# ScalarE in place of SyncE as the issuer of the crossbar transposes in the second FFN

## The chip, the core and the metric

The kernel runs on one core of a Trainium2 chip. The metric is the device time of one execution in microseconds (us). The engines are TensorE (PE, with its weight loads listed apart as PEld), VectorE (DVE), ScalarE (ACT), GpSimd (POOL) and SyncE (SP). Each works through its own instructions in order, and they wait for one another by semaphores. DMAs are issued by an engine's instruction and carried out by 16 DMA engines.

## What is computed

One conformer-like block in float32 on 256 tokens of width 2048: a feed-forward network (FFN), a mixer of differential attention and a causal convolution, and a second FFN. Each is normalised, scaled and shifted with values computed from `c` and `w_ada`.

```
def swiglu(h, w_gu, w_down):
    gu = jnp.einsum('bsd,df->bsf', h, w_gu)
    g, u = jnp.split(gu, 2, axis=-1)
    return jnp.einsum('bsf,fd->bsd', jax.nn.silu(g) * u, w_down)
...
ada = jnp.einsum('bd,de->be', c_act, w_ada[l]) + b_ada[l]
sh1, sc1, g1, shm, scm, gm, sh2, sc2, g2 = jnp.split(ada, N_MOD, axis=-1)
...
h = modulate(rms_norm(x, ffn2_norm[l]), sh2, sc2)
x = x + FFN_RESIDUAL_WEIGHT * g2[:, None, :] * swiglu(h, ffn2_w_gu[l], ffn2_w_down[l])
```

The hidden width of an FFN is 5632. The change is in the second FFN.

## The kernel before

**Weights.** All weights come from memory as float32 tiles of 128 x 2048 (1 MB), which SP loads into the four buffers `raw` (L294, L542). `w_tile` splits each half of a tile into a high and a low part: ACT casts it to `whi` (L305), DVE subtracts to get `wlo` (L307); both have four buffers. `mm3` then makes three matmuls for each product: high times high (L329), high times low (L333), low times high (L334). Half a tile is used by 12 matmuls of 512 columns. So PE needs an ACT cast and a DVE subtraction for every 12 matmuls, and a buffer comes free for the next cast when its 12 matmuls are done.

**The first half of the second FFN.** The 5632 hidden columns are cut into 22 chunks of 256 gate and 256 up columns. The products of a chunk's first of four tiles are made ahead and kept in `parts` (chunks 3, 4 and 5 two of four); the rest are made by a loop over `groups`, first chunks 0, 1 and 2 together, then one chunk at a time, three tiles each (chunks 3, 4 and 5 two). When a chunk's matmuls are done, and the first tile of the next group has been put out, `finish` runs for both token halves: DVE adds the two sums (L830), ACT takes the SiLU (L831), DVE multiplies by the up half (L832).

**The transposes.** The products must be transposed before they can be the stationary operand of the second half. The first FFN does it on PE (`CROSSBAR[0]` is False). The second (`CROSSBAR[96]` is True) uses the DMA engines: ACT splits the product's 32-bit words into two planes of 16 bits (L836, tile `planes`); one tile of instructions later, `rest` has a DMA transpose all eight 128 x 128 blocks of a chunk at once into `turned` (L842); ACT puts the planes together again (L845), casts to the high part (L350), and DVE subtracts to get the low part (L351). In the profile `planes`, `turned` and the result of L845 are all called `tmp`. So each chunk has a line of dependent work L830, L831, L832, L836, L842, L845, L350, L351 over DVE, ACT, the DMA engines, ACT and DVE.

**Fillers.** The remaining `w_ada` rows are loaded into the same `raw` buffers (L192) and reduced on DVE (L193), one for every two weight tiles while any are left (to about 1465 us).

**The order.** The order of each engine's instructions is fixed when the program is built, by a scheduler that simulates the engines with its own costs, in the order and with the priorities in which the code is written. Which engine issues a DMA is part of what it schedules, so moving an issue can move other instructions as well. The second half of the FFN (`down_strassen`) starts after the last chunk.

Of the kernel before, what the change touches and what calls it, by code (L numbers as in the profile page):

```python
# [82 lines left out]
def block_kernel(ctx: ExitStack, tc: tile.TileContext, x_in, pos_in, w_ada, small, w_gu1, w_dn1,  # L83
                 w_in, w_out, w_gu2, w_dn2, out):
    nc = tc.nc
# [18 lines left out]
    def blk(shape, dtype=F32):  # L104
        return blkp.tile(shape, dtype, tag="blk", name=nm("blk"))

    def tmp(shape, dtype=F32):
        return tmpp.tile(shape, dtype, tag="tmp", name=nm("tmp"))
# [7 lines left out]
    def tp_tile(shape=(P, 512)):  # L116
        return tpp.tile(list(shape), F32, tag="tp", name=nm("tp"))
# [53 lines left out]
    def after_tiles(n, fn):  # L171
        later.append([n, fn])
# [176 lines left out]
    def split_from_psum(tp, hi, lo):  # L349
        nc.scalar.copy(out=hi, in_=tp)  # L350
        nc.vector.tensor_sub(out=lo, in0=tp, in1=hi.bitcast(F32))  # L351
# [287 lines left out]
    def ffn(st, w_gu, w_dn, gate_base, ada_a, ada_b, nxt, again, early, early_3):  # L639
# [187 lines left out]
        def finish(c, accs):  # L827
            p = parts[c]
            for t in range(NT):
                nc.vector.tensor_add(out=p[:, t, :], in0=accs[t], in1=p[:, t, :])  # L830
                nc.scalar.activation(out=p[:, t, :256], in_=p[:, t, :256], func=AF.Silu)  # L831
                nc.vector.tensor_mul(out=p[:, t, 256:], in0=p[:, t, :256], in1=p[:, t, 256:])  # L832

            if CROSSBAR[base]:
                planes = tmp([P, 2, NT, 256], U16)
                nc.scalar.copy(out=planes, in_=p[:, :, 256:].bitcast(U16).rearrange("p t (f b) -> p b t f", b=2))  # L836

            def rest():
                a = blk([P, 2, 2, S], F32R)
                if CROSSBAR[base]:  # L840
                    turned = tmp([P, 2, NT, 2, P], U16)
                    nc.sync.dma_start_transpose(out=turned.rearrange("p b t i s -> p (b t i) s"),  # L842
                                                in_=planes.rearrange("p b t f -> p (b t f)"))
                    src = tmp([P, 2, NT, P])
                    nc.scalar.copy(out=src.bitcast(U16).rearrange("p i t (s b) -> p b t i s", b=2), in_=turned)  # L845
                    src = src.rearrange("p i t s -> p i (t s)")
                else:
                    src = tp_tile((P, 2, S))
                    for t in range(NT):
                        for i in range(2):  # L850
                            nc.tensor.transpose(src[:, i, t * P:(t + 1) * P],
                                                p[:, t, 256 + i * P:256 + (i + 1) * P], ident)
                split_from_psum(src, a[:, 0], a[:, 1])
                aT[c] = a

            after_tiles(1, rest)
# [613 lines left out]
```

## Time and profile before

| | |
|---|---|
| runs before: median, lowest, highest | 1826.58, 1826.22, 1826.65 us |
| profiled execution: time, and span from first to last instruction | 1831.11, 1829.3 us |
| granted TensorE clock, mean | 0.999 |
| L842 in the profile | 22 issues by SP, first at 1295.3, last at 1596.8 us |
| ACT, L845 in all | 22, mean 1355 ns, 51.2 us of idle time ahead of them |
| ACT casts of weights (L305) | 581, mean 1044 ns (nearly all 128 x 1024) |
| DVE subtractions (L307) | 581, mean 1210 ns |
| DVE reduction of a `w_ada` row (L193) | 142, mean 2285 ns |

Times in the profile's views are us from the span's start. A row of the order of time gives start, length, engine, line, operation, tile written and tiles read, and in brackets how long the engine stood idle before it and what ended that; rows with x2 or x3 put instructions of one kind that follow each other together. PE's matmuls are pipelined, so their lengths overlap.

### The profile page before, as it was taken

What the parts mean: (1) busy time and instruction counts of PE and PEld (TensorE: products, weight loads), DVE (VectorE), ACT (ScalarE), POOL (GpSimd) and SP (SyncE); (2) the same over time, 40 slices, a digit from 0 to 9 for tenths busy, and PEclk for the clock granted to TensorE, in tenths of its full rate; (3) what the DMA queues carried; (4) which work ended last, traced back from release to release, by engine and by line L of the source; (5) the groups of instructions that cost most, each with busy time, mean ns of one, the idle gap of its engine ahead of it and who ended that gap; (6) DMA issues with size and microseconds to landing.
All of it is one profiled execution on the core that took longest, in us unless ns stands there. A gap on an engine that the chain in (4) does not pass through costs nothing.

```text
span 1829.3 us, 21896 instructions
## 1 busy us (share of the span) xinstructions
PE 1802.8 (99%) x8117; PEld 1484.0 (81%) x8117; DVE 1519.9 (83%) x2018; ACT 1008.3 (55%) x1521; POOL 28.3 (2%) x29
## 2 busy tenths in 40 slices
PE   7999999999999999999999999999999999999998
PEld 5788888888888887788888787888888888878887
DVE  6889869999898787898999778878887765699877
ACT  6553444444444344566798655664665565555453
POOL 0000000000000000000110100000000000000000
PEclk9999999999999999999999999999999999999999
DMA  9987978888889998775444466889899877655552
GB/s 373 349 307 297 347 274 310 327 314 337 337 330 350 355 343 327 290 261 206 176 147 162 160 254 241 328 337 346 262 313 298 302 242 222 203 207 210 204 214 109
DMA packets 95962, 501.68 MB, mean 274 GB/s; under 512 B 31424, under 2 KB 31856, under 8 KB 38384
## 3 DMA queue, kind: packets, MB, share of 16 engines
q1 hardware_dynamic: 95856, 500.30, 74.4%
q8 instruction: 63, 1.03, 0.2%
q14 instruction: 43, 0.35, 0.1%
HBM read 492.37 MB, written 2.12 MB: 270 GB/s over the span
## 4 chain that ended last, share of the span: by engine, by line
PE 85%; DVE 6%; DMA 4%; ACT 3%; issue 2%; POOL 0%; POOLq 0%; DVEq 0%; SPq 0%; ACTq 0%
PE acc L333 27%; PE acc L334 27%; PE acc L329 27%; DVE wlo L307 2%; DMA tmp<-tmp 1%; DMA xall<-in_x_dram 1%; PE tp L333 1%; PE tp L334 1%; DMA raw<-in_w_ada_dram 1%; PE tp L329 1%; ACT whi L305 1%; PE acc L1137 1%; DVE raw L193 1%; DVE wlo L513 1%; DVE blk L1029 1%
## 5 line engine op out<-in xcount | busy, mean ns | idle before, releaser
L333 PE MATMUL acc<-wlo,blk 128*128 128x512 f32 x2340 | 913.7, 390 | 6.9 <-DVE wlo L307 6.9
L329 PE MATMUL acc<-whi,blk 128*128 128x512 f32 x2343 | 911.4, 392 | 1.9 <-ACT blk L403 1.4
L334 PE MATMUL acc<-whi,blk 128*128 128x512 f32 x2340 | 912.3, 390 | 0.1
L305 ACT CAST whi<-raw 128x1024 fp32r<-128x1024 f32 (+1 forms) x581 | 597.3, 1044 | 473.3 <-PE acc L334 333.9
L307 DVE TENSOR_TENSOR wlo<-raw,whi 128x1024 fp32r<-128x1024 f32 (+1 forms) x581 | 691.1, 1210 | 177.7 <-ACT whi L305 176.6
L333 PEld LDWEIGHTS acc<-wlo,blk 128*128 128x128 f32 x2340 | 439.6, 188 | 103.1 <-DVE wlo L307 12.9
L329 PEld LDWEIGHTS acc<-whi,blk 128*128 128x128 f32 x2343 | 439.9, 188 | 93.4 <-ACT blk L403 1.8
L334 PEld LDWEIGHTS acc<-whi,blk 128*128 128x128 f32 x2340 | 439.3, 188 | 91.9 <-DVE blk L405 0.7
L193 DVE CUSTOM_DVE_ANT_0 raw<-raw,c_bc 128x2048 f32<-128x2048 f32 x142 | 324.2, 2285 | 10.3 <-DMA raw<-in_w_ada_dram 10.3
L512 ACT CAST whi<-raw 128x1024 fp32r<-128x1024 f32 (+1 forms) x56 | 53.0, 947 | 68.4 <-PE tp L334 31.9
L513 DVE TENSOR_TENSOR wlo<-raw,whi 128x1024 fp32r<-128x1024 f32 (+1 forms) x56 | 60.8, 1087 | 19.1 <-ACT whi L512 18.9
L666 ACT COPY blk<-acc 128x512 f32<-128x512 f32 x72 | 42.0, 590 | 62.9 <-PE acc L334 60.2
L1029 DVE SCALAR_TENSOR_TENSOR blk<-blk,cst,blk 128x245 f32<-128x245 f32 (+21 forms) x176 | 70.4, 457 | 0.6 <-ACT blk L1027 0.5
L845 ACT COPY tmp<-tmp 128x1024 uint16<-128x1024 uint16 x22 | 29.8, 1355 | 51.2 <-DMA tmp<-tmp 51.2
L830 DVE TENSOR_TENSOR blk<-acc,blk 128x512 f32<-128x512 f32 x88 | 56.6, 682 | 0.0
L831 ACT ACTIVATE blk<-blk 128x256 f32<-128x256 f32 x88 | 33.7, 413 | 20.5 <-DVE blk L830 20.4
L329 PE MATMUL acc<-blk,blk 128*128 128x512 f32 x104 | 41.3, 401 | 1.2 <-ACT blk L321 1.2
L333 PE MATMUL acc<-blk,blk 128*128 128x512 f32 x100 | 39.1, 391 | 0.6 <-DVE blk L307 0.6
L334 PE MATMUL acc<-blk,blk 128*128 128x512 f32 x100 | 39.0, 392 | 0.0
L351 DVE TENSOR_TENSOR blk<-tmp,blk 128x512 fp32r<-128x512 f32 x22 | 15.1, 688 | 26.0 <-ACT blk L350 26.0
L832 DVE TENSOR_TENSOR blk<-blk 128x256 f32<-128x256 f32 x88 | 33.8, 417 | 0.4 <-ACT blk L831 0.4
L836 ACT COPY tmp<-blk 128x1024 uint16<-128x1024 uint16 x22 | 22.9, 1042 | 14.2 <-DVE blk L832 14.1
(227 smaller groups left out, 1058.7 us busy)
## 6 DMA issues: line engine op xcount, KB each, us to landing
raw<-in_w_gu_dram SPq DMA_DIRECT2D x161, 1024.0 KB, 6.0
raw<-in_w_ada_dram SPq DMA_DIRECT2D x142, 1024.0 KB, 6.3
raw<-in_w_dn_dram SPq DMA_DIRECT2D x88, 1024.0 KB, 5.4
raw<-in_w_in_dram SPq DMA_DIRECT2D x40, 1024.0 KB, 4.8
raw<-in_w_out_dram SPq DMA_DIRECT2D x16, 1024.0 KB, 4.8
raw<-in_w_gu_dram SPq DMA_DIRECT2D x8, 768.0 KB, 6.5
blk<-in_w_gu_dram SPq DMA_DIRECT2D x10, 512.0 KB, 13.5
blk<-gate_line SPq DMA_DIRECT2D x6, 512.0 KB, 4.8
```

Source lines behind the costliest of these rows:

```text
L193: nc.vector.tensor_tensor_reduce(out=raw, in0=raw, in1=c_bc, scale=1.0, scalar=0.0, op0=ALU.mult, op1=ALU.add, accum_out=ada_cols[g][:, j ...
L305: nc.scalar.copy(out=hi[:, :m, :], in_=rw)
L307: nc.vector.tensor_sub(out=lo[:, :m, :], in0=rw, in1=hi[:, :m, :].bitcast(F32))
L329: nc.tensor.matmul(acc, ah, wh, start=start, stop=False)
L333: nc.tensor.matmul(acc, ah, wl, start=False, stop=False)
L334: return nc.tensor.matmul(acc, al, wh, start=False, stop=stop)
L512: nc.scalar.copy(out=hi[:, :n, :], in_=src)
L513: nc.vector.tensor_sub(out=lo[:, :n, :], in0=src, in1=hi[:, :n, :].bitcast(F32))
L666: last_part[0] = nc.scalar.copy(out=parts[c][:, t, :], in_=accs[t])
L830: nc.vector.tensor_add(out=p[:, t, :], in0=accs[t], in1=p[:, t, :])
L832: nc.vector.tensor_mul(out=p[:, t, 256:], in0=p[:, t, :256], in1=p[:, t, 256:])
L1029: nc.vector.scalar_tensor_tensor(out=y[:, d:], in0=u, scalar=w, in1=y[:, d:], op0=ALU.mult, op1=ALU.add)
```

## The change

In the second FFN, ACT issues the DMA transpose in place of SP. Tiles, sizes and all other code stay.

```diff
@@ -839,7 +839,7 @@
                 a = blk([P, 2, 2, S], F32R)
                 if CROSSBAR[base]:
                     turned = tmp([P, 2, NT, 2, P], U16)
-                    nc.sync.dma_start_transpose(out=turned.rearrange("p b t i s -> p (b t i) s"),
+                    nc.scalar.dma_start_transpose(out=turned.rearrange("p b t i s -> p (b t i) s"),
                                                 in_=planes.rearrange("p b t f -> p (b t f)"))
                     src = tmp([P, 2, NT, P])
                     nc.scalar.copy(out=src.bitcast(U16).rearrange("p i t (s b) -> p b t i s", b=2), in_=turned)
```

The order changes with it. These rows are ACT's at chunks 0 to 2, from the last of their three L836 on (- before, + now; `whi` and `raw` are weights, `tmp` the planes and their transposes):

```order
 L836 COPY tmp_10687<-blk_9232 128x1024
+L842 DMA_TRANSPOSE tmp_10724<-tmp_10671 128x8x128
 L305 CAST whi_10752<-raw_10750 128x1024
 L305 CAST whi_10756<-raw_10750 128x1024
 L845 COPY tmp_10726<-tmp_10724 128x2x2x2x128
+L842 DMA_TRANSPOSE tmp_10731<-tmp_10679 128x8x128
 L350 CAST blk_10723<-tmp_10726 128x512
 L305 CAST whi_10794<-raw_10792 128x1024
 L845 COPY tmp_10733<-tmp_10731 128x2x2x2x128
```

The second transpose stands behind the L845 that reads the first, and the third, which follows these rows, behind the second's L845.

The next rows are ACT's at chunk 7, from its L836 on:

```order
 L836 COPY tmp_11216<-blk_9487 128x1024
+L842 DMA_TRANSPOSE tmp_11253<-tmp_11216 128x8x128
 L305 CAST whi_11268<-raw_11262 128x1024
+L845 COPY tmp_11255<-tmp_11253 128x2x2x2x128
 L305 CAST whi_11300<-raw_11298 128x1024
-L845 COPY tmp_11255<-tmp_11253 128x2x2x2x128
 L350 CAST blk_11252<-tmp_11255 128x512
 L305 CAST whi_11304<-raw_11298 128x1024
```

The transpose stands right behind L836, and L845 one cast earlier than before. It is so for chunks 4 to 13; from chunk 14 on, L845 stood there before too, and only the transpose is new.

The last rows are SP's in the same place:

```order
 L294 DMA raw_11344<-in_w_gu_dram 128x2048
-L842 DMA_TRANSPOSE tmp_11253<-tmp_11216 128x8x128
 L294 DMA raw_11385<-in_w_gu_dram 128x2048
 L192 DMA raw_11420<-in_w_ada_dram 128x2048
```

SP keeps the loads in their order, without the transpose between them. On DVE, in every other of these chunks, the second L832 now follows the first directly, behind the subtraction that stood between them, and an L193 stands one subtraction earlier; PE's matmuls keep their order but for one place in the second half.

## The prediction

> **What bounds the kernel now.** I read the page first, then busy times by stretch, then who waits for whom in the stretch of the change, then the order of time there.
>
> ```profile
> PE 1802.8 (99%) x8117; PEld 1484.0 (81%) x8117; DVE 1519.9 (83%) x2018; ACT 1008.3 (55%) x1521; POOL 28.3 (2%) x29
> ...
> 1290.00:1466.00 176.00, 174.85 (x768) 143.60 (x768) 141.28 (x167) 107.68 (x128) 0.00 (x0) 1.00 0.91 300
> 1466.00:1605.00 139.00, 139.00 (x616) 114.99 (x615) 84.67 (x99) 83.28 (x97) 0.00 (x0) 1.00 0.67 219
> ```
>
> The first row is the page's busy time by engine. The other two are stretches from 1290 to 1605 us, which hold all 22 transposes; after the length stand PE, PEld, DVE, ACT and POOL busy (with counts), granted clock, DMA share and GB/s. PE is the bound: it idles 1.15 us in the first stretch and nothing in the second. So the change can give back at most about 1.2 us; it can cost more, if PE is made to wait. What differs between the stretches is the filling work: in the first, DVE also reduces `in_w_ada` tiles (L193) and the DMA engines are 91% busy, in the second neither.
>
> ```profile
> PE acc L333 <- DVE wlo L307: 1.2, 2, 0.8
> ACT tmp L845 <- DMA tmp<-tmp: 32.5, 13, 4.3
> ACT blk L831 <- DVE blk L830: 18.3, 16, 3.3
> DVE blk L351 <- ACT blk L350: 22.7, 8, 4.8
> DVE raw L193 <- DMA raw<-in_w_ada_dram: 4.7, 8, 0.9
> ...
> ACT whi L305 <- PE acc L334: 27.0, 24, 1.7
> ```
>
> These are waits (us, times, longest): five rows of 1290 to 1466, and the last of 1466 to 1605. In the later stretch ACT waits 24 times for PE to free a `whi` buffer: its casts run as far ahead as the four buffers let them. In the earlier one, that wait is nearly gone, and ACT and DVE wait for each other and for the transposes: 32.5 us of ACT stand before L845, 22.7 us of DVE before L351. There a loop of dependent work runs, from one chunk's L836 to the next chunk's L836, and it sets how far ahead of PE the casts are.
>
> **The loop, on one chunk.**
>
> ```profile
> 1419.44 1.04 ACT L836 COPY tmp<-blk 128x1024 uint16<-128x1024 uint16 x1 [2.11 <-DVE blk L832]
> 1420.40 2.00 ACT L305 CAST whi<-raw 128x1024 fp32r<-128x1024 f32 x2
> 1424.90 1.35 ACT L845 COPY tmp<-tmp 128x1024 uint16<-128x1024 uint16 x1 [2.50 <-DMA tmp<-tmp]
> 1426.28 0.62 ACT L350 CAST blk<-tmp 128x512 fp32r<-128x512 f32 x1
> 1433.09 0.42 ACT L831 ACTIVATE blk<-blk 128x256 f32<-128x256 f32 x1 [3.17 <-DVE blk L830]
> 1435.49 1.05 ACT L836 COPY tmp<-blk 128x1024 uint16<-128x1024 uint16 x1 [0.44 <-DVE blk L832]
> ...
> 1420.52 1.24 SPq L842 DMA_TRANSPOSE tmp<-tmp  x1
> ...
> 1420.60 0.50 PE L333 MATMUL acc<-wlo,blk 128*128 128x512 f32 x1 [0.79 <-DVE wlo L307]
> ...
> 1426.93 0.69 DVE L351 TENSOR_TENSOR blk<-tmp,blk 128x512 fp32r<-128x512 f32 x1 [2.91 <-ACT blk L350]
> 1427.88 1.22 DVE L307 TENSOR_TENSOR wlo<-raw,whi 128x1024 fp32r<-128x1024 f32 x1 [0.26 <-ACT whi L305]
> 1429.03 2.28 DVE L193 CUSTOM_DVE_ANT_0 raw<-raw,c_bc 128x2048 f32<-128x2048 f32 x1
> 1432.37 1.28 DVE L830 TENSOR_TENSOR blk<-acc,blk 128x512 f32<-128x512 f32 x2
> 1433.90 1.22 DVE L307 TENSOR_TENSOR wlo<-raw,whi 128x1024 fp32r<-128x1024 f32 x1
> ```
>
> Start, length, engine, line, and in brackets the idle time ahead. L836 ends near 1420.4; SP issues the transposes at 1420.52; ACT makes two casts and stands idle 2.50 us until they have landed; L845, L350, then DVE's L351, which stood 2.91 us, and behind it in DVE's order a `wlo` subtraction, L193, another subtraction and L830 of the next chunk; ACT's L831 waits for that, and the next L836 starts at 1435.49, 16.05 us after the last. PE had caught up at 1420.60.
>
> **The change, part by part.** It moves 22 issues from SP to ACT. Nothing is computed differently, and the matmuls keep their number.
>
> *Issue time.*
>
> ```profile
> L842 SPq DMA_TRANSPOSE tmp<-tmp x22: 1237/1239/2462, 1295.3 to 1596.8; - x22
> DMA to landing us min/median/max: 3.3/4.5/8.8
> ...
> DMA to landing us min/median/max: 4.5/7.8/8.8
> DMA to landing us min/median/max: 3.5/4.7/6.2
> DMA to landing us min/median/max: 3.3/3.5/4.7
> ```
>
> The first row is min/median/max of the issue in ns; the landings are of all 22, then of the first 4, the next 8 (1339 to 1452 us) and the last 9. On SP an issue takes 1.24 us; no row shows one on ACT. Its bounds are nothing and the slowest on SP, 2.46 us; I take 1.24, the median of the same operation: 22 x 1.24 = 27.3 us of ACT. It lies inside the landing: issue and one cast are 1.24 + 0.95 = 2.2 us (2.46 + 0.95 = 3.4 at the upper bound), under the median landing of 4.5. Cost: nothing. Without that cover it would be 1.24 us a chunk.
>
> *The place of L845.* In the new order of the middle chunks one cast stands between L836's transposes and L845, where two stood. The second now comes behind L845 and ahead of L350. In the loop above that cast ran inside the idle 2.50 us; now it runs after the landing, with L350, L351 and all that DVE has behind L351 queued behind it: +0.95 us a turn (half of the 2.00 us of two casts, which overlap a little).
>
> What a turn may take:
>
> ```profile
> 1337.93 1.05 ACT L836 COPY tmp<-blk 128x1024 uint16<-128x1024 uint16 x1 [0.48 <-DVE blk L832]
> 1467.59 1.05 ACT L836 COPY tmp<-blk 128x1024 uint16<-128x1024 uint16 x1 [0.44 <-DVE blk L832]
> ...
> 1524.07 1.05 ACT L305 CAST whi<-raw 128x1024 fp32r<-128x1024 f32 x1 [1.05 <-PE acc L334]
> 1526.79 1.05 ACT L305 CAST whi<-raw 128x1024 fp32r<-128x1024 f32 x1 [1.67 <-PE acc L334]
> ```
>
> Between the first two rows lie 8 turns: 129.66 / 8 = 16.21 us. The other two are successive buffers freed by PE: 2.72 us for half a tile, so 6 x 2.72 = 16.32 us for a chunk of three tiles. The loop has 0.11 us to spare a turn. The landing on ACT's queue no row shows. Bounds: 3.5 (last 9) and 6.2 (worst of the middle 8). I take 4.5, the median of all, close to the 4.7 of this stretch, since the loads it shares the DMA engines with stay: -0.2 a turn. So the loop falls behind PE by 0.95 - 0.2 - 0.11 = 0.64 us a turn, 8 x 0.64 = 5.1 us. From this goes the lead the casts have. PE took up the late half at 1420.60; the subtraction of the row at 1433.90 feeds the sixth half after it, due at 1420.60 + 6 x 2.72 = 1436.92, and ended at 1435.12, 1.8 us early. In the new order it stands ahead of both L832, not between them, 0.3 us earlier. Lead 2.1; **+3.0 us**. At 3.5 us of landing the loop closes, and PE's 1.2 us of waiting could vanish (-1.2); at 6.2 it is 8 x 2.34 - 2.1 = +16.6.
>
> *The first three chunks.*
>
> ```profile
> 1298.71 1.05 ACT L836 COPY tmp<-blk 128x1024 uint16<-128x1024 uint16 x1 [0.49 <-DVE blk L832]
> 1301.64 1.05 ACT L305 CAST whi<-raw 128x1024 fp32r<-128x1024 f32 x1 [0.94 <-PE acc L334]
> 1310.12 1.99 ACT L305 CAST whi<-raw 128x1024 fp32r<-128x1024 f32 x2
> 1314.27 1.35 ACT L845 COPY tmp<-tmp 128x1024 uint16<-128x1024 uint16 x1 [2.15 <-DMA tmp<-tmp]
> ...
> 1321.17 0.50 PE L333 MATMUL acc<-wlo,blk 128*128 128x512 f32 x1 [0.36 <-DVE wlo L307]
> ```
>
> SP issued their transposes from 1295.29 on, one while the last was in flight. On ACT each issue but the first stands behind the L845 of the one before: issue, land, copy, in turn. From the end of the last L836 (1299.7), with 4.5 us to land and 1.25 for the copy, the third L845 starts at 1299.7 + 3 x 4.5 + 2 x 1.25 = 1315.7, against 1314.27. That is late by 1.4 alone, but the second cast of the row at 1310.12 now stands behind it, behind L836, L350 and the fourth issue: 1315.7 + 1.25 + 0.95 + 0.5 + 1.24 = 1319.6. The cast at 1301.64 began as its buffer came free, three halves or 8.16 us ahead of use, at 1309.8; the one in question is due three halves later, 1318.0. Done at 1320.6, its `wlo` 1.2 later, 1321.8: PE's second matmul of that half, wanted at 1318.2, starts 3.6 us late. Before, PE lost 0.4 here, so **+3.2 us**. Bounds: at 3.5 us the chain is 3 us shorter, +0.2; at the 7.8 that these transposes took on SP, 9.9 longer, +13.
>
> *SP.* The loads behind its transposes issue up to 1.24 us and a wait for L836 earlier. ACT and PE show no wait for `in_w_gu` loads up to 1466; DVE waited 4.7 us for `in_w_ada`. Bounds 0 and -4.7; I take 0, since SP's `in_w_ada` issues stood mostly for a `raw` buffer that DVE frees. *The last 9 chunks:* L845 already stood behind one cast (in all but the first of them), ACT leads by whole buffers, and 1.24 us fit into them: 0 (1.24 each if the lead were gone, 11 us).
>
> **Sum:** +3.0 + 3.2 = +6.2 us on the profiled execution's 1831.1, so 1837.3. The median of the runs is 4.5 us lower: **1832.8**.
>
> [...]
>
> **Rivals.** *1. Not slower: the landing shortens.* On SP the transposes wait behind weight loads in the same queue: the landing falls from 7.8 through 4.7 to 3.5 us as the DMA load falls. On a queue that holds nothing else it could be 3.5 to 4.0 everywhere. From 4.0 down the loop closes (0.95 - 0.7 - 0.11 = 0.1 a turn, within the lead), the first chunks cost 1.7 or less, and the end is -1 to +2: 1825.5 to 1828.5. For: the 7.8. Against: in the middle stretch 91% of the DMA engines' time is taken, in whatever queue the bytes wait.
> [...]
> *2. The landing lengthens.* [...] At 5.0 to 6.2 us the middle costs +7 to +17 and the first chunks +4.7 to +8.3: 1838 to 1851. Against: two queues don't add bytes.
> *3. The order hides it.* ACT and DVE could regain the cast's 0.95 us where the loop now idles, such as the 0.5 us before some L193. Then +1 to +3: 1827.5 to 1829.5, inside rival 1's outcome for the chances.
> That the change would do nothing is excluded: all 22 issues stand on ACT in the new order.
>
> **How the numbers follow.** Forecast (landing 4.2 to 5.0, 1829.5 to 1838): 0.52. Rivals 1 and 3: 0.34. Rival 2: 0.14. From what PE idles, a gain of more than 1.2 us has no source in this stretch; 0.03 stands for the unforeseen. A measurement tells apart about 0.2%, 3.7 us here. Slower by more: rival 2 and most of the forecast, 0.14 + 0.43 = 0.57; within: 0.40; faster: 0.03. The range takes in rival 1 and the lower part of rival 2: 1825.5 to 1841.
>
> **What would show it.** PE's idle time between 1290 and 1470 at 6 to 8 us instead of 1.2, all of it before L333 for `wlo`; L836 to L836 at 16.7 to 17 us; L842 at 1.24 us on ACT; landings near 4.5; after 1470 no PE wait. Landings under 4.0, or a first stretch without a PE wait near 1318, would make it wrong downward; landings over 5, or PE waits in the last 9 chunks, upward.

## The result and the profile after

| | before | after |
|---|---|---|
| median of the runs, us | 1826.45 | 1884.72 |
| lowest and highest | 1826.22, 1826.65 | 1882.44, 1888.64 |
| profiled execution, us | 1831.11 | 1882.96 |
| mean granted clock | 0.999 | 0.988 |

The ratio is 1.0321, with an interval of 1.0306 to 1.0336: 58 us slower, against the 6 us forecast. The sign was right, the size was not, and the time lies outside the range.

The page's busy time by engine, of after:

```profile
PE 1818.3 (97%) x8117; PEld 1491.2 (79%) x8117; DVE 1519.0 (81%) x2018; ACT 1007.4 (54%) x1521; POOL 28.3 (2%) x29
```

Two stretches of after, with the columns used before (length; PE, PEld, DVE, ACT, POOL; clock, DMA share, GB/s):

```profile
1290.00:1466.00 176.00, 148.53 (x596) 117.30 (x594) 105.92 (x127) 83.78 (x99) 0.00 (x0) 0.91 0.80 231
1466.00:1605.00 139.00, 128.24 (x551) 104.20 (x551) 85.22 (x99) 75.87 (x89) 0.00 (x0) 0.98 0.71 221
```

DVE's and ACT's work is what it was (1519 and 1007 us); PE's grew by 15.5 us without one more matmul. From 1290 to 1605 PE stands still for 27.47 + 10.76 = 38.2 us, and from there to 1660 not at all. Before, it was 1.15 up to 1466 and nothing up to 1605.

The clock fell as well. There are five stretches at half clock between 1290 and 1660 us; three of them, and the sum of all five:

```profile
1315.60:1322.40 6.80, 5.74 (x13) 4.17 (x14) 6.14 (x9) 5.20 (x6) 0.00 (x0) 0.50 0.63 168
1332.70:1342.90 10.20, 6.58 (x15) 4.87 (x16) 8.26 (x10) 6.62 (x9) 0.00 (x0) 0.50 0.56 200
...
1506.70:1513.60 6.90, 4.14 (x9) 2.97 (x10) 4.62 (x5) 5.60 (x6) 0.00 (x0) 0.51 0.03 12
sum 37.50, PE 25.15 PEld 18.23 DVE 28.70 ACT 27.20 POOL 0.00; mean PE 5.03 PEld 3.65 DVE 5.74 ACT 5.44 POOL 0.00
```

PE worked 25.15 us of these 37.5 at a clock of 0.50, so about half of that work, 12.6 us, is by this estimate an effect of the clock. Added idle time and clock together, 37.1 + 12.6, are 49.7 of the 52 us between the two profiled executions. Each of the five stretches begins within a stop of PE, of 2.88, 6.16, 5.16, 6.56 and 7.22 us in turn; the first stop began at 1313.31 us, and the clock fell 2.3 us after its start.

What PE waited for, from the waits between 1285 and 1660 us (total, times, longest):

```profile
DVE wlo L307 <- ACT whi L305: 118.4, 53, 12.0
ACT tmp L845 <- DMA tmp<-tmp: 87.3, 21, 11.0
...
PE acc L329 <- ACT whi L305: 29.4, 6, 7.2
...
PE acc L333 <- DVE wlo L307: 8.6, 11, 2.2
```

PE waits for weight casts, the casts stand on ACT behind the copy L845, and L845 waits for the transposes: 87.3 us, where the whole program before had 51.2. The chain of waits from 1290 to 1500 us says it in one line each, for before and for after:

```profile
by line: PE acc L333 24.2%; PE acc L334 23.6%; PE acc L329 23.6%; DMA tmp<-tmp 11.1%; DMA raw<-in_w_ada_dram 6.5%; issue 4.1%; ACT tmp L845 1.9%; DVE wlo L307 1.7%; DVE raw L193 1.6%; ACT whi L305 0.5%; DVE blk L351 0.3%; ACT blk L350 0.3%;
```

```profile
by line: DMA tmp<-tmp 49.6%; issue 15.2%; DVE wlo L307 10.9%; DVE raw L193 5.3%; DVE blk L830 5.1%; ACT tmp L836 4.6%; ACT whi L305 4.5%; DVE blk L832 3.8%; DVE blk L351 1.9%; ACT tmp L845 1.3%; ACT blk L350 0.7%; ACT blk L831 0.3%; DVE ada
```

Matmuls were 71% of it; now half is transposes under way. The issue itself is as forecast, the landing is not. The instructions of L842 in after, all 22 (ns), their landings, and below these the landings of those from 1335 to 1470 us (min, median, max):

```profile
L842 ACTq DMA_TRANSPOSE tmp<-tmp x22: 1247/1249/1583, 1296.9 to 1648.4; - x22
DMA to landing us min/median/max: 3.1/5.8/13.5
...
DMA to landing us min/median/max: 4.7/7.5/12.7
```

In that stretch the median was 4.6 and the maximum 6.2 before. Two chunks of after in the order of time, of ACT, then SP, then PE, show one long and one shorter landing:

```profile
1412.94 1.25 ACTq L842 DMA_TRANSPOSE tmp<-tmp  x1
1425.62 1.33 ACT L845 COPY tmp<-tmp 128x1024 uint16<-128x1024 uint16 x1 [10.34 <-DMA tmp<-tmp]
1438.38 1.25 ACTq L842 DMA_TRANSPOSE tmp<-tmp  x1
1444.28 1.35 ACT L845 COPY tmp<-tmp 128x1024 uint16<-128x1024 uint16 x1 [3.55 <-DMA tmp<-tmp]
...
1413.04 0.33 SPq L192 DMA_DIRECT2D raw<-in_w_ada_dram  x1
1416.57 15.71 SPq L294 DMA_DIRECT2D raw<-in_w_gu_dram  x2
1443.86 0.33 SPq L192 DMA_DIRECT2D raw<-in_w_ada_dram  x1
...
1427.90 0.80 PE L329 MATMUL acc<-whi,blk 128*128 128x512 f32 x1 [6.56 <-ACT whi L305]
```

At 1412.94 ACT issues the transposes, and SP issues a 1 MB `w_ada` load 0.10 us later, on its own queue, and a weight load at 1416.57. The copy starts 12.7 us after the issue, and PE has stood still for 6.56 us. At 1438.38 the `w_ada` load comes 5.5 us behind, and the copy starts after 5.9. Before, both were SP's, from the order of time of before:

```profile
1386.59 1.24 SPq L842 DMA_TRANSPOSE tmp<-tmp  x1
1387.94 0.51 SPq L192 DMA_DIRECT2D raw<-in_w_ada_dram  x1
```

The issue of the transposes, 1.24 us, kept the two apart, and the load stood behind the transposes in one queue: from the first to the last packet of these transposes (1388.93 to 1392.23 us, 3.3 us) 13 packets of 8 KB, those of loads, moved. In after, 157 did from the first to the last packet of those issued at 1412.94 (1416.31 to 1424.46 us, 8.2 us). What these two chunks of after show holds for all 22. The eight landings of 7.5 us and more are those for which SP issued a load between 0.13 us before and 1.4 us behind the transposes; beside the other fourteen it issued none in that time, and they took 3.1 to 6.2 us.

### The profile page after: what moved, and what is told of

The parts are those of the page before. It is cut to its first block, busy times and chain, and to the rows that moved or that the text cites. A ratio compares the mean times of both kernels' runs of the same rounds, so it can differ in the third digit from the quotient of the medians.

```text
span 1881.2 us, 21880 instructions
## 1 busy us (share of the span) xinstructions
PE 1818.3 (97%) x8117; PEld 1491.2 (79%) x8117; DVE 1519.0 (81%) x2018; ACT 1007.4 (54%) x1521; POOL 28.3 (2%) x29
## 4 chain that ended last, share of the span: by engine, by line
PE 77%; DVE 9%; DMA 6%; issue 4%; ACT 4%; POOL 0%; SPq 0%; POOLq 0%; DVEq 0%; ACTq 0%
PE acc L333 24%; PE acc L334 24%; PE acc L329 24%; DMA tmp<-tmp 6%; DVE wlo L307 3%; ACT whi L305 1%; DVE raw L193 1%; PE tp L333 1%; PE tp L334 1%; PE tp L329 1%; DVE blk L830 1%; ACT tmp L836 1%; PE acc L1137 1%; DVE wlo L513 1%; DVE blk L1029 1%
## 5 line engine op out<-in xcount | busy, mean ns | idle before, releaser
L329 PE MATMUL acc<-whi,blk 128*128 128x512 f32 x2343 | 917.0, 394 | 31.3 <-ACT whi L305 29.6
L333 PE MATMUL acc<-wlo,blk 128*128 128x512 f32 x2340 | 919.5, 393 | 14.5 <-DVE wlo L307 14.4
L305 ACT CAST whi<-raw 128x1024 fp32r<-128x1024 f32 (+1 forms) x581 | 597.0, 1044 | 487.3 <-PE acc L334 317.1
L329 PEld LDWEIGHTS acc<-whi,blk 128*128 128x128 f32 x2343 | 442.8, 189 | 127.0 <-ACT whi L305 33.9
L333 PEld LDWEIGHTS acc<-wlo,blk 128*128 128x128 f32 x2340 | 442.0, 189 | 115.3 <-DVE wlo L307 24.6
L193 DVE CUSTOM_DVE_ANT_0 raw<-raw,c_bc 128x2048 f32<-128x2048 f32 x142 | 324.3, 2285 | 15.9 <-DMA raw<-in_w_ada_dram 15.8
L845 ACT COPY tmp<-tmp 128x1024 uint16<-128x1024 uint16 x22 | 29.6, 1347 | 87.3 <-DMA tmp<-tmp 87.3
L329 PE MATMUL acc<-blk,blk 128*128 128x512 f32 x104 | 41.3, 400 | 1.1 <-ACT blk L321 1.1
L333 PE MATMUL acc<-blk,blk 128*128 128x512 f32 x100 | 39.0, 390 | 0.0
L832 DVE TENSOR_TENSOR blk<-blk 128x256 f32<-128x256 f32 x88 | 33.5, 419 | 0.2 <-ACT blk L831 0.2
L307 DVE TENSOR_TENSOR blk<-raw,blk 128x1024 fp32r<-128x1024 f32 x24 | 28.8, 1219 | 1.0 <-ACT blk L305 1.0
```

What stands on the lines that cost most here:

```text
L193: nc.vector.tensor_tensor_reduce(out=raw, in0=raw, in1=c_bc, scale=1.0, scalar=0.0, op0=ALU.mult, op1=ALU.add, accum_out=ada_cols[g][:, j ...
L305: nc.scalar.copy(out=hi[:, :m, :], in_=rw)
L307: nc.vector.tensor_sub(out=lo[:, :m, :], in0=rw, in1=hi[:, :m, :].bitcast(F32))
L329: nc.tensor.matmul(acc, ah, wh, start=start, stop=False)
L333: nc.tensor.matmul(acc, ah, wl, start=False, stop=False)
```

## The experiments

Each time is compared with that of the kernel before on the same chip. Two theories stood at the start: **Q**, that transposes on a second queue land later when loads are under way on the first; and **O**, that the new order on ACT (one cast instead of two ahead of L845) is the cost. Runs 1 and 12 were built to set them apart, but neither has throughout the order that it was built for; where they depart from it is said there.

**1. The new order, SP still issuing.** From the kernel before; the cast of the second tile after a transpose is put behind the copy L845 (L848 here).

```diff
+            joined[1] += h == 0
+            with tc.issue_after(joined[0].ins) if joined[0] and joined[1] == 2 and h == 0 else nullcontext():
+                nc.scalar.copy(out=hi[:, :m, :], in_=rw)
...
```

> SP issues the transposes as before; ACT's copies and casts stand in the order of the changed kernel (one cast behind L845). Theory O, the order costs: most of the 58 us come back, 1860 us or more. Theory Q, the second DMA queue costs: landings stay near 4.7 us in the middle chunks, and the time is 1826 to 1833, a cast per chunk at most.

Measured: 1839.23 us, 1.0063 times the 1827.32 of before (1.0048 to 1.0078): +12, between the two expectations. Its first stretch:

```profile
1290.00:1466.00 176.00, 168.35 (x723) 136.82 (x722) 129.88 (x155) 100.28 (x117) 0.00 (x0) 0.97 0.84 280
```

The copy that ends a turn of the loop (L836 in the kernel before), at the start of a turn and eight turns later:

```profile
1340.32 1.04 ACT L839 COPY tmp<-blk 128x1024 uint16<-128x1024 uint16 x1
1475.48 1.05 ACT L839 COPY tmp<-blk 128x1024 uint16<-128x1024 uint16 x1 [0.44 <-DVE blk L835]
```

The landings from 1335 to 1470 us:

```profile
DMA to landing us min/median/max: 4.1/5.1/6.2
```

These are near the 4.6 of before. Eight turns of the loop take 135.16 us, 16.9 each, as the prediction said. PE idles 7.65 us, and the clock of 0.97 adds some 5 us (0.03 x 176), which the prediction did not price. But nearly all of this comes from one place ahead of these turns, in the order of time of ACT and PE:

```profile
1311.80 1.33 ACT L848 COPY tmp<-tmp 128x1024 uint16<-128x1024 uint16 x1 [4.09 <-DMA tmp<-tmp]
1314.45 2.93 ACT L308 CAST whi<-raw 128x1024 fp32r<-128x1024 f32 x3
1315.55 1.22 PE L332 MATMUL acc<-whi,blk 128*128 128x512 f32 x2 [5.82 <-ACT whi L308]
1317.44 1.22 PE L332 MATMUL acc<-whi,blk 128*128 128x512 f32 x2 [0.68 <-ACT whi L308]
```

Here no cast stands between 1299.99 and 1314.45 us: the edit put all of them behind the third copy. The changed kernel has a cast behind each of the first two copies. From 1335 to 1605 us, where run 1's order is the changed kernel's, PE idles 1.7 us, at full clock. So the 12 us are not a measure of the order; in the middle chunks it cost little here, with PE already late.

**2. ACT issuing, the copy far off; 3. the same with SP issuing.** L845 and the two steps behind it are written three tiles (a whole chunk of the loop) later, so that ACT does not stand before them. The diff is the same for both; 2 starts from the changed kernel, 3 from the one before.

```diff
-                    src = tmp([P, 2, NT, P])
-                    nc.scalar.copy(out=src.bitcast(U16).rearrange("p i t (s b) -> p b t i s", b=2), in_=turned)
-                    src = src.rearrange("p i t s -> p i (t s)")
+                    after_tiles(3, lambda: join(a, turned))
+                    return
...
```

> ACT issues the transposes as in the changed kernel, but the copies L845 and L350 that wait for a chunk's landing are written three tiles later, so that in the single chunks they stand a whole chunk (16 us) behind the issue. If the cost reaches PE only because ACT stands and waits for a long landing: landings stay long (median over 5 us, some over 9), L845 hardly waits, 1824 to 1835 us, granted clock 0.998 or more. If the interleaving also costs PE by making the weight loads late: 1845 or more, with casts or L193 waiting for raw tiles. If the issue on ACT costs by itself (22 x 1.25 us): 1850 or more without such waits.

> The control of the run with ACT's late copies: SP issues, the copies three tiles later. Both theories: 1824 to 1828 us, PE's 1.2 us of waiting at most to gain; it shows what the later copies do by themselves.

Measured: 1832.32 us with ACT (ratio 1.0031, 1.0013 to 1.0049) and 1826.8 with SP (0.9996, 0.9987 to 1.0006). The landings from 1335 to 1470 us, of run 2 and then of run 3:

```profile
DMA to landing us min/median/max: 6.0/7.1/8.9
```

```profile
DMA to landing us min/median/max: 4.1/4.3/6.3
```

The first stretch of run 2:

```profile
1290.00:1466.00 176.00, 174.68 (x770) 144.01 (x769) 140.30 (x168) 107.16 (x126) 0.00 (x0) 1.00 0.93 297
```

On its own queue the transposes take nearly as long at the median as in the changed kernel, 7.1 us against 7.5, though the copy is out of the way; the longest took 8.9 us against 12.7. PE idles only 1.3 us. So the landing is long because of the queue, and most of the 58 us are there because ACT waits for it in order with the casts behind. The 5.5 us between the two medians do not show in the profiled execution of run 2, which took 1828.79 us; its runs spread from 1827.83 to 1841.53, and what the longer ones lost is not shown.

**4. A load held back.** From the changed kernel: SP first copies a few bytes out of the landed tile, so that a load behind it is issued after the landing (from the fourth chunk on).

```diff
+                    landed = dramp.tile([16, 4], U16, name=nm("landed"))
+                    gates[w_count[0] + 4] = nc.sync.dma_start(out=landed, in_=turned[:16, 0, 0, 0, :4])
...
```

> ACT issues as in the changed kernel; from the fourth chunk on SP, ahead of the load that stood behind the transposes before, issues a small DMA that reads the transposed tile, so that SP waits for the landing before it issues further loads. Theory Q: in chunks 3 to 13 the landings get shorter (none over 8 us, median under 5), and a good part of the 58 us goes, 1835 to 1870, less what SP's wait costs. Theory O or the issue on ACT: landings as in the changed kernel, 1880 or more, since only a wait is added.

Measured: 1875.29 us (ratio 1.0257, 1.0236 to 1.0279), between the two expectations. The longest landing falls from 13.5 to 9.2 us and L845's wait from 87.3 to 64.1. PE's wait before the matmul with `whi` falls from 29.4 to 13.0 us, but that before the matmul with `wlo` grows from 8.6 to 19.6. One load was held, others were under way: the four transposes with a `w_ada` load 0.1 to 0.4 us behind them landed in 7.5 to 8.6 us, where the changed kernel, with the next weight load 3.6 us behind as well, has 7.5 to 13.3. This suggests that each of the two loads has a part in the long landings. How much of the loss they make, this run doesn't settle.

**5. The loads on another queue, transposes on SP.** From the kernel before: GpSimd issues the `w_gu` and `w_ada` loads of this half.

```diff
-            w_dma[0] = nc.sync.dma_start(out=raw[:, :n, :], in_=src[:, k0:k0 + n, :])
+            w_dma[0] = loader[0].dma_start(out=raw[:, :n, :], in_=src[:, k0:k0 + n, :])
...
+        if CROSSBAR[base]:
+            loader[0] = nc.gpsimd
```

> The kernel before, with one edit on the other side of the pair: SyncE keeps the crossbar transposes, and from the start of the second FFN's first half to its end GpSimd, not SyncE, issues the loads of w_gu and of the w_ada rows. ACT's order and its instructions are those of before. Transposes and loads are on two queues, as in the changed kernel, with no part of it on ACT. Theory Q (a transpose that is under way on one queue while 8 KB load packets are on another takes far longer than 4.7 us to land, and the loads beside it slow down): median issue to landing above 5 us, the longest above 9, the cast L845 waits over 40 us in all, PE in 1290 to 1466 idle for 10 us or more, total 1840 to 1890. Rival (the issue on ACT and its order are the cost, two queues are not): landings as in before, about 4.5, total 1825 to 1832.

Measured: 1898.2 us (ratio 1.0381, 1.0359 to 1.0403). The landings of its transposes from 1335 to 1470 us:

```profile
DMA to landing us min/median/max: 5.9/10.5/16.9
```

ACT issues nothing here, and still the landings double and more (10.5 us at the median, 4.6 before): transposes on one queue and loads on another are enough. ACT's order is not the old one, though. From the fourth chunk on one cast stands ahead of the copy, as in the changed kernel from the fifth on (L837, L306 and L846 are L836, L305 and L845 here):

```profile
1357.48 1.05 ACT L837 COPY tmp<-blk 128x1024 uint16<-128x1024 uint16 x1 [1.51 <-DVE blk L833]
1358.43 1.04 ACT L306 CAST whi<-raw 128x1024 fp32r<-128x1024 f32 x1
1375.50 1.33 ACT L846 COPY tmp<-tmp 128x1024 uint16<-128x1024 uint16 x1 [16.03 <-DMA tmp<-tmp]
```

So it speaks for the landing and not against the order. Its loss, over the 1890 expected, isn't a measure of the change either, since the loads are GpSimd's here and wait in its order.

**6 and 7. Short rows.** Every load in four DMAs of 512 columns, 2 KB a row, with ACT and with SP issuing the transposes.

```diff
-            w_dma[0] = nc.sync.dma_start(out=raw[:, :n, :], in_=src[:, k0:k0 + n, :])
+            for k in range(n):
+                w_dma[0] = nc.sync.dma_start(out=raw[:, k:k + 1, :], in_=src[:, k0 + k:k0 + k + 1, :])
```

> The changed kernel, with every load of weights and of w_ada rows in the whole program made as four DMAs of 512 columns each (2 KB a row in place of 8 KB), the same bytes to the same places. [...]

> Control for the run with small loads: the kernel before with the same four DMAs of 512 columns for each load, transposes on SyncE. Both theories: within 1% of before (1815 to 1845); it gives the base that the run with the transposes on ACT is held against.

Measured: 1918.54 us with ACT, 1868.55 with SP, beside 1828.07 of before. The control is 2.2% slower than before, outside what was expected. From its sixth chunk on it too has one cast ahead of the copy, so its 40 us hold what the new order costs, and the loss against it, 1918.54 - 1868.55 = 50 us, is that of the second queue in the new order. It is to be held against 58 - 12 = 46, the changed kernel against run 1, as well as against 58. All 22 landings, ACT first, then SP:

```profile
DMA to landing us min/median/max: 4.2/6.6/13.0
```

```profile
DMA to landing us min/median/max: 3.0/5.4/6.7
```

With rows of 2 KB in place of 8 KB, the landings with ACT (6.6 us at the median, against 5.8 in the changed kernel) and the loss are nearly what they were. So theory Q holds with the shorter rows too: the landings are 1.2 us longer at the median with ACT issuing than with SP, and the longest 13.0 against 6.7.

**8 and 9. Fewer loads.** In this half the `w_ada` loads are left out, with ACT and with SP issuing the transposes; DVE's reduction of these tiles stays.

```diff
+        if quiet[0]:
+            nc.gpsimd.memset(raw, 0.0)
+        else:
+            nc.sync.dma_start(out=raw, in_=w_ada[j])
...
```

> The changed kernel with fewer loads beside the transposes: from the start of the second FFN's first half to its end the w_ada rows (about 1 MB each, some 16 of them) aren't loaded; GpSimd writes zeros to their buffers in place of the load, so those modulation values are zero. The w_gu loads stay. Theory Q (loads in flight on the other queue stretch the transposes): the landings of 10 us and more, which in the changed kernel stood in every second chunk, beside a w_ada load, go: longest landing under 8.5, median under 5.5, L845's wait from 87 to under 45 us, and the loss against the run beside it (same loads left out, SyncE issuing) falls from 58 to 10 to 30 us. If the loss comes from ACT's issue and order alone, it stays over 45.

> Control for the run with fewer loads: the kernel before with the same w_ada loads left out (GpSimd writes zeros in their place, so those modulation values are zero), transposes on SyncE. Both theories: 1815 to 1835, landings as in before or shorter, 3 to 5 us.

Measured: 1852.8 us with ACT, 1828.14 with SP: the loss falls from 58 to 25 us. The median landing, all 22, is 3.6 us with ACT against 5.8 in the changed kernel; the longest is 16.6, where under 8.5 was expected, and L845 waits 58.8 us, where under 45 was. More than half of the loss needs the `w_ada` loads beside the transposes. But it isn't these loads as such: six landings of run 8 took 7.1 to 16.6 us, each with a weight load issued 0.1 to 1.2 us behind the transposes, and the others at most 5.4. In the control the scheduler put one cast ahead of every other copy from the seventh chunk on, with no loss, and the landings there were 3.1 to 4.6 us.

**10 and 11. The first three and the last nine.** ACT issues the transposes of some chunks only.

```diff
-                    nc.scalar.dma_start_transpose(out=turned
+                    (nc.scalar if c < 3 else nc.sync).dma_start_transpose(out=turned
```

> One part of the change alone: ACT issues the transposes of the first three chunks only, SyncE those of the other nineteen. The prediction put 3.2 us on the first three (their steps run one after the other on ACT), 3.0 on the rest. If the first three are a small term, 1828 to 1833. If much of the 58 us starts there (in the changed kernel PE stood idle or at half clock for over 10 us of the 40 behind 1310 us), 1838 to 1855. Theory Q puts more on the chunks that follow than on these three.

> The other end of the change alone: ACT issues the transposes of the last nine chunks, behind the last w_ada load beside a chunk; SyncE those of the first thirteen. The prediction put these nine at nothing (ACT leads PE by whole buffers there, and 1.24 us a chunk fit into that): 1825 to 1829, landings of the nine 3.3 to 4.7 as in before, no PE wait. Theory Q by itself, if the mere presence of a second queue beside the w_gu loads stretches a landing to 7 us or more: median landing of the nine over 5, and 1829 to 1840.

(The second has `c >= 13`.) Measured: 1836.19 us for the first three (ratio 1.0042, 1.0025 to 1.0059), +8.3 and between the two expectations; and 1827.8 for the last nine, 1.000 (0.999 to 1.001). The landings of run 11's nine, with ACT issuing:

```profile
DMA to landing us min/median/max: 3.4/3.4/4.6
```

Their stretch:

```profile
1466.00:1605.00 139.00, 139.00 (x616) 114.99 (x615) 84.87 (x100) 81.28 (x96) 0.00 (x0) 1.00 0.65 210
```

The same issue on the same second queue lands as on SP's here, where the DMA engines are 65% busy and SP issues its next load 3.6 us or more behind the transposes. In these nine a second queue alone did no harm; the landings of 7.5 us and more in after are those with a load issued at nearly the same moment, from 0.13 us before to 1.4 us behind the transposes.

**12. ACT issuing, the old order.** From the changed kernel; the copy is put behind the second cast.

```diff
+            hi_cast = nc.scalar.copy(out=hi[:, :m, :], in_=rw)
+            if joins and h == 0:
+                joins[0][0] -= 1
+                if joins[0][0] == 0:
+                    with tc.issue_after(hi_cast.ins):
+                        joins.pop(0)[1]()
...
```

> The fourth cell of a table of two by two: ACT issues the transposes, and the copy L845 (L846 here) stands on ACT behind two weight casts, as in the kernel before, in place of one. The other three: SyncE with before's order 1826.5, SyncE with the new order 1839.2, ACT with the new order 1884.7. Theory Q (the second queue is the larger part by itself): 1850 to 1880, median landing over 4.7 and the longest over 9, the cast's wait 50 us or more. If the two causes only hurt together (the queue lengthens a wait that the order alone has put on the path): 1828 to 1842.

Measured: 1847.18 us (ratio 1.0108, 1.0091 to 1.0125), between the two expectations.

| loss, us | built for the old order on ACT | new order on ACT |
|---|---|---|
| SP issues | 0 | 12 (run 1) |
| ACT issues | 19 (run 12) | 58 |

The two causes would make 31 us one by one and 58 together, as if about half of the loss were there only because a longer landing meets an order with less cover. But the 12 and the 19 both hold orders of their own, so this isn't shown. In run 12 three transposes stand one behind the other, without a copy between, and their issue held ACT, as the order of time of ACT shows:

```profile
1297.16 11.16 ACTq L854 DMA_TRANSPOSE tmp<-tmp  x3
1308.42 3.88 ACT L306 CAST whi<-raw 128x1024 fp32r<-128x1024 f32 x4 [10.22 <-issue]
```

PE idles 11.6 us from 1290 to 1660 in this run, 4.1 of them behind this stall. And the three copies that this left over put off those that follow, since the edit lets one go at every second tile. Up to 1405 us a copy stands behind six or more casts, not two. Here the copy that follows an issue at 1.3 us, less than any landing took, is that of the chunk before:

```profile
1356.95 1.25 ACTq L854 DMA_TRANSPOSE tmp<-tmp  x1
1358.24 1.35 ACT L846 COPY tmp<-tmp 128x1024 uint16<-128x1024 uint16 x1 [1.32 <-issue]
```

So the middle chunks up to there are more like those of run 2. With two casts ahead of the copy, from 1400 to 1485 us, PE idles 5.6 us and its clock is 0.96: a longer landing costs something in the old order too. How the 58 us divide between the landing and the order stays open.

No version beat the kernel before: the best, run 3, is level with it, and PE's idle time there leaves nothing to gain.

## Why the prediction was wrong

- **PE as the bound, nothing to gain: right.** Nothing ran faster.
- **The issue on ACT, 1.24 us and hidden: right.** The median is 1.249 us. Nine of them on ACT cost nothing where the landings stayed short (run 11), and with all 22 on ACT and the copies late PE idled 1.3 us in the first stretch (run 2).
- **The order's term: right in its turns, not shown in its cost.** Forecast were 6 to 8 us of idle time and turns of 16.7 to 17; run 1 has 7.65 us and 16.9. The turns bear the loop out. The idle time agrees by luck: 6.5 us of it are one stop near 1316 us, from casts that the changed kernel has elsewhere. All of it was to be before the matmul with `wlo` (L333); in the changed kernel PE waited 22.1 us before the matmul with `whi` (L329) and 5.1 before L333 up to 1466.
- **The clock: taken at nothing.** In after, PE's clock fell to one half in each of five stops of 2.9 to 7.2 us, for 6.8 to 10.2 us, which costs some 12.6 us by the estimate above. This term was missing in the sum everywhere.
- **The first three chunks: the amount was right by luck.** PE was to be 3.6 us late near 1318 us, at the cast behind the third L845, behind L836, L350 and the fourth issue. It waited 2.88 + 0.47 us there, but one cast earlier, at the cast behind the second L845, as the order of time of ACT and PE in after shows:

```profile
1312.60 1.34 ACT L845 COPY tmp<-tmp 128x1024 uint16<-128x1024 uint16 x1 [5.16 <-DMA tmp<-tmp]
1315.11 1.03 ACT L305 CAST whi<-raw 128x1024 fp32r<-128x1024 f32 x1
1316.05 1.34 ACT L845 COPY tmp<-tmp 128x1024 uint16<-128x1024 uint16 x1
1316.19 0.79 PE L329 MATMUL acc<-whi,blk 128*128 128x512 f32 x1 [2.88 <-ACT whi L305]
1317.45 0.79 PE L333 MATMUL acc<-wlo,blk 128*128 128x512 f32 x1 [0.47 <-DVE wlo L307]
1318.32 1.25 ACTq L842 DMA_TRANSPOSE tmp<-tmp  x1
1331.86 1.33 ACT L845 COPY tmp<-tmp 128x1024 uint16<-128x1024 uint16 x1 [10.20 <-DMA tmp<-tmp]
```

  The first two landings took 7.6 and 8.1 us in place of 4.5, and the third only 3.1, with no load beside it, so the third copy did not wait. Issue, landing and copy in turn were right; the landing, again, was the wrong input. Meanwhile the clock halved, and the fourth chunk's transposes took 13.5 us. Run 10 gives 8.3 us for the three alone, against 3.2.
- **The landing on ACT's queue, taken as 4.5 us: this is the step that failed.** The reason given was that "the loads it shares the DMA engines with stay". They stay, but not where they were: in the two chunks above, 13 of their packets moved between the first and the last packet of the transposes with one queue, and 157 with two. Before, a `w_ada` load issued 1.35 us behind left the landing at 4.4 to 6.2 us; in after, one issued 0.1 us behind went with 7.5 to 13.3. The landing was 7.5 us in the middle chunks. Put into the prediction's own formula, this gives a turn of 16.21 + 0.95 + (7.5 - 4.7) = 19.96 us; L836 to L836 took (1474.97 - 1337.77) / 7 = 19.6 us. So the loop was right and its input wrong. Rival 2 had the direction, but bounded the landing by the worst that one queue had shown, 6.2, and got a chance of 0.14 because "two queues don't add bytes".
- **SP's relief, taken as 0 with a gain as its only other end: wrong in sign.** That SP's loads go out 1.24 us earlier is how the `w_ada` load came to be issued 0.10 us behind the transposes. Leaving these loads out takes 33 us of the loss away (runs 8 and 9).
- **The last nine chunks, taken as 0: right.** Run 11 shows no loss, and in after the first of the nine is issued at 1519.55 us, behind which PE waits 0.77 us up to 1605. The sign that was named, no PE wait after 1470, failed all the same: PE idled 10.8 us behind 1466, since the chunks before these nine were late and the `w_ada` loads ran on to 1493 us. The last chunk with such a load, the thirteenth, in the order of time of ACT and PE in after:

```profile
1493.38 1.25 ACTq L842 DMA_TRANSPOSE tmp<-tmp  x1
1506.71 1.33 ACT L845 COPY tmp<-tmp 128x1024 uint16<-128x1024 uint16 x1 [10.99 <-DMA tmp<-tmp]
1508.99 0.80 PE L329 MATMUL acc<-whi,blk 128*128 128x512 f32 x1 [7.22 <-ACT whi L305]
```

That the landing is longer because transposes and loads are on two queues is shown by runs 2, 3 and 5, and that it costs because ACT waits for it in order by runs 2 and 3; the halved clock is read from the trace. What stays open: how the loss divides between the landing and the new order on ACT, since runs 1 and 12 don't separate them; how the DMA engines divide their time between transposes and loads; and why a load issued at nearly the same moment made one landing 7.1 us long and another 16.6 (run 8).

## What to carry to other kernels

Here a short DMA whose landing is waited for landed in 4.6 us (median of the middle chunks) in the queue that it shared with long loads, and in 7.5 us on a queue beside theirs. Before such a DMA is moved to another engine's queue, look in the order of time for what the old queue will issue at the same moment, and bound its landing by more than the worst seen in one queue. Where the waiting engine has other work behind the wait, use the landed data a stage later: that made the longer landing nearly free here (1832.3 against 1884.7 us).

## What the runs showed of the hardware

- Transposes of 256 KB that landed in 3.4 to 4.6 us when no load was issued within 3.6 us behind them (run 11) took 7.5 to 13.5 us in after with a load issued on another queue from 0.13 us before to 1.4 us behind them. The loads suffered too: the weight load issued 1.4 us behind the fourth chunk's transposes took 14.5 us, where the median of all is 5.9. In that stretch of after, the DMA engines were fully taken and moved little:

```profile
1320.00:1331.00 11.00, 7.98 (x30) 6.10 (x29) 3.25 (x4) 1.66 (x2) 0.00 (x0) 0.89 1.12 117
```

  117 GB/s at a share of 1.12 (the share adds up the packets' times, so it can pass 1), against 300 at 0.91 before, in the first stretch.
- Three transposes issued back to back on ACT took 11.16 us to issue, in place of 3 x 1.25 (run 12).
- In after, the clock fell to one half in each of PE's five stops of 2.9 to 7.2 us, for 6.8 to 10.2 us; of 52 us between the profiled executions some 12.6 are this, by the estimate above.
